# Sliding-window attention in blocks of 64 queries by 192 keys, late scores in the projections' banks, and other ends of the program

## The chip, the cores and the metric

One core of a Trainium2 chip runs the whole program. The metric is device microseconds (us) of one execution; lower is better. Engines are named as in the profile: PE does matmuls and transposes (PEld is its weight load), DVE and ACT the elementwise work, POOL a little elementwise work and some DMA issues, SP most DMA issues. The inputs and outputs lie in DRAM; PE writes into PSUM banks, everything else that is worked on lies in SBUF.

## What is computed

A step of a two-layer decoder in fp32, for a prompt of 1024 tokens and for 8 single tokens with caches (1032 columns in all, model width 1024). Layer 0 is gated linear attention beside attention into 256 memory tokens, then a squared-ReLU MLP. Layer 1, in which most of the change lies, is sliding-window attention beside memory attention, then the MLP. Its core, cut:

```
nb = L // WINDOW                                   # WINDOW = 128, L = 1024: 8 blocks
qb = q.reshape(B, nb, WINDOW, 4, 3, 64)            # 12 query heads on 4 key heads of 64
kk, vv = band_keys(k), band_keys(v)                # each block sees itself and the block before: 256 keys
qi = arange(WINDOW)[:, None] + WINDOW; kj = arange(2 * WINDOW)[None, :]
dist = qi - kj
band = (dist >= 0) & (dist < WINDOW)               # a query sees the 128 keys that end with its own
s = q . k / 8 + bias[dist], -inf outside the band
m = max(max_k s, sink);  p = exp(s - m);  p = p / (sum_k p + exp(sink - m));  o = p . v
```

A query in the first half of a block of 128 can see only the first 192 of the 256 keys, one in the second half only the last 192. The single tokens attend to a cache of 127 keys and their own, and the cache, shifted by one, is also an output.

## The kernel before, in words

Work is laid out with features on partitions and tokens on columns; the 1032 tokens go in three chunks `c` (`CH`: 384, 384 and 264 columns). A projection (`proj`, matmul at L248) is done in three fp32r products of high and low parts; `mmps` hands out its PSUM banks ("mm", "mx"). A scheduler sets the order on each engine from the priorities written in the code (`first()` raises one by 400) and from when buffers come free.

Layer 1's window attention is `swa(t, i2)` (L1713 to L1773): `t` counts 6 pairs of heads, `i2` 4 pairs of 128-token blocks, 24 calls, here called units and written (t, i2). A unit has: four score matmuls of 64 rows by 128 columns with 256 keys each (L1726) into the double bank `sA`, of which there is one; on DVE four `tensor_tensor_reduce` that add the bias and take the maximum into `z` (L1730), and small ones (L1735, L1737); on ACT the sink's exponential (L1740) and four exponentials (L1745); the sum and its reciprocal (L1747, L1749) and one multiplication of 128x1024 (L1751) on DVE; eight transposes on PE into `sT` (L1758, one buffer); their copy `pt` on ACT (L1760); eight matmuls with the values `vtok` into bank `sf` (L1769, "PV" below); one copy into `q` on ACT (L1773). A trace shows an fp32 matmul as two passes, so that L1769 is x16 and L1726 x8. Units with i2 = 0 have no block before their first one, and leave out a quarter of this.

The loop (L1865 to L1877) calls `in_b(t)`, the query projection for pair t (L1704, 72 matmuls), before the four units of pair t, and `in_b(5)` before those of pair 3. So from pair 4 on no projection is left to fill PE between units. From unit (4, 2) on, each unit is preceded by a step of `swa_dec` (L1775), the single tokens' attention: its loads from POOL's queue (L1780 to L1784, L1806, L1808), the shifted copy of the key and value caches from DRAM to DRAM (L1785, L1786), the memory attention's loads (L444) and scores (L454), window scores (L1817) and values (L1846). After the units come the output projection (L496 on) and layer 1's MLP.

At the start of the program the first chunk of `xT` and the first weights are loaded (L1019, L214), normalised and split (L1030, L1031, L152), for the first projection matmuls (L248). At its end, `down_plain` (L976) does the MLP's second half; `Residual` collects each chunk's sum of squares, and its `finish` (L286) makes the factor `rf` (L192, the statistics' matmul L198, ACT, L207 to L209), then in four pieces j multiplies by it (L320), adds the residual that was loaded from `xd` (L322) and stores (L323).

## Time and profile before

| | us |
|---|---|
| median of 3 runs | 2208.44 |
| lowest and highest | 2204.39, 2211.3 |
| the profiled execution's own time | 2209.21 |
| its span in the trace | 2207.4 |
| PE busy | 2152.1 (97%) |
| DVE, ACT, POOL busy | 1504.0, 1061.5, 109.4 |

The span is the time from the first to the last recorded instruction of the profiled execution; its own time is 1.8 us more. Times within the trace count from the span's start. A busy share is a mean over stages that have different limits, so the stages are read one by one below.

### The profile page before, as it was taken

The page shows a single profiled execution, that of the slowest core. Times are in us where ns is not written, and L with a number is a line of the kernel's source. Part 1 is how long each engine was busy: PE and PEld are TensorE (multiplying, and loading weights), DVE is VectorE, ACT ScalarE, POOL GpSimd, SP SyncE. Part 2 cuts the span into 40 slices and gives each one's busy share as a digit, 9 for nine tenths or more (in the row PEclk, how much of TensorE's full clock was granted, in tenths as well). Part 3 has the DMA queues.
Part 4 walks back from the last instruction along what each step waited for, and adds up shares of the span by engine and source line. Part 5 has one row for each costly group of instructions (what it writes and reads, how often), then busy time and mean ns, then how long its engine had stood idle before and what let it go on. Part 6 is the DMA issues. An engine that isn't in the chain of part 4 may idle for free.

```text
span 2207.4 us, 40137 instructions
## 1 busy us (share of the span) xinstructions
PE 2152.1 (97%) x16250; PEld 2054.4 (93%) x16250; DVE 1504.0 (68%) x2811; ACT 1061.5 (48%) x2071; POOL 109.4 (5%) x123
## 2 busy tenths in 40 slices
PE   7999999999999999999999999799999999999996
PEld 5879999999999999999999778599999999999996
DVE  6656647768877777666478465647887776856557
ACT  6354536557644554334334365646654544433433
POOL 0002000000000002520000000100000000000010
PEclk9999999999999999999999999899999999999998
DMA  5512016543644459574334101324364337635422
GB/s 186 161 63 80 24 64 168 163 131 106 200 157 159 138 196 337 176 256 128 111 95 140 48 20 40 106 73 145 112 219 158 128 138 264 220 112 167 149 88 78
DMA packets 134687, 303.68 MB, mean 138 GB/s; under 512 B 11033, under 2 KB 65489, under 8 KB 134209
## 3 DMA queue, kind: packets, MB, share of 16 engines
q1 hardware_dynamic: 116736, 258.80, 36.0%
q0 software_dynamic: 7824, 29.44, 3.8%
q10 hardware_dynamic: 9936, 12.81, 1.6%
q8 instruction: 129, 2.11, 0.4%
q14 instruction: 62, 0.51, 0.1%
HBM read 213.57 MB, written 89.51 MB: 137 GB/s over the span
## 4 chain that ended last, share of the span: by engine, by line
PE 84%; DVE 4%; ACT 2%; DMA 2%; issue 1%; DVEq 0%; ACTq 0%
PE mm L248 15%; PE mx L248 7%; PE mx L756 6%; PE mx L758 6%; PE mx L757 6%; PE mx L921 4%; PE mx L923 4%; PE mx L922 4%; PE mm L756 3%; PE mm L758 3%; PE mm L757 3%; PE mm L922 2%; PE mm L921 2%; PE mm L923 2%; PE sx L921 1%; PE sf L922 1%
## 5 line engine op out<-in xcount | busy, mean ns | idle before, releaser
L152 ACT CAST wh<-ws 128x512 fp32r<-128x512 f32 (+1 forms) x262 | 188.3, 726 | 319.7 <-DVE ws L605 105.7
L153 DVE TENSOR_TENSOR wl<-ws,wh 128x512 fp32r<-128x512 f32 (+1 forms) x262 | 213.7, 822 | 122.8 <-ACT wh L152 121.7
L756 PE MATMUL mx<-xf,wh 128*128 128x258 f32 x1048 | 297.1, 283 | 0.0
L758 PE MATMUL mx<-xf,wl 128*128 128x258 f32 x1048 | 295.9, 282 | 0.0
L757 PE MATMUL mx<-xf,wh 128*128 128x258 f32 x1048 | 295.7, 282 | 0.0
L248 PE MATMUL mm<-xh,wh 128*128 128x384 f32 (+1 forms) x864 | 282.0, 326 | 0.8 <-ACT xh L152 0.5
L248 PE MATMUL mm<-xh,wl 128*128 128x384 f32 (+1 forms) x864 | 278.9, 323 | 0.0
L248 PE MATMUL mm<-xl,wh 128*128 128x384 f32 (+1 forms) x864 | 278.7, 323 | 0.0
L152 ACT CAST wh<-wr 128x1024 fp32r<-128x1024 f32 x98 | 103.0, 1051 | 315.3 <-PE sx L922 300.3
L153 DVE TENSOR_TENSOR wl<-wr,wh 128x1024 fp32r<-128x1024 f32 x98 | 119.8, 1223 | 173.7 <-ACT wh L152 173.7
L921 PE MATMUL mx<-sa,wh 128*128 128x258 f32 x784 | 221.6, 283 | 1.1 <-DVE aw L594 1.1
L922 PE MATMUL mx<-sa,wh 128*128 128x258 f32 x784 | 220.6, 282 | 0.0
L923 PE MATMUL mx<-sa,wl 128*128 128x258 f32 x784 | 220.5, 282 | 0.0
L757 PEld LDWEIGHTS mx<-xf,wh 128*128 128x128 f32 x1048 | 198.1, 189 | 0.4
L756 PEld LDWEIGHTS mx<-xf,wh 128*128 128x128 f32 x1048 | 197.7, 189 | 0.4
L758 PEld LDWEIGHTS mx<-xf,wl 128*128 128x128 f32 x1048 | 197.9, 189 | 0.0
L248 PEld LDWEIGHTS mm<-xh,wh 128*128 128x128 f32 x864 | 163.0, 189 | 10.8 <-issue 6.3
L248 PEld LDWEIGHTS mm<-xh,wl 128*128 128x128 f32 x864 | 162.6, 188 | 7.4 <-issue 5.4
L248 PEld LDWEIGHTS mm<-xl,wh 128*128 128x128 f32 x864 | 163.2, 189 | 6.5 <-issue 5.5
L921 PEld LDWEIGHTS mx<-sa,wh 128*128 128x128 f32 x784 | 147.5, 188 | 1.6 <-DVE aw L594 1.5
L922 PEld LDWEIGHTS mx<-sa,wh 128*128 128x128 f32 x784 | 148.4, 189 | 0.0
L923 PEld LDWEIGHTS mx<-sa,wl 128*128 128x128 f32 x784 | 148.1, 189 | 0.0
(542 smaller groups left out, 5749.6 us busy)
## 6 DMA issues: line engine op xcount, KB each, us to landing
ra<-awd SPq DMA_DIRECT2D x98, 516.0 KB, 3.9
ws<-in_w_up SPq DMA_DIRECT2D x64, 512.0 KB, 6.1
wr<-in_w_downb SPq DMA_DIRECT2D x56, 512.0 KB, 5.6
awd<-aw SPq DMA_DIRECT2D x26, 1032.0 KB, 6.8
awd<-am SPq DMA_DIRECT2D x28, 774.0 KB, 8.3
ws<-in_w_in_a SPq DMA_DIRECT2D x20, 512.0 KB, 3.6
xd<-f ACTq DMA_DIRECT2D x24, 384.0 KB, 4.8
ws<-in_w_out SPq DMA_DIRECT2D x16, 512.0 KB, 3.5
```

Source lines behind the costliest of these rows:

```text
L152: nc.scalar.copy(hi, src)
L153: (eng or nc.vector).tensor_tensor(lo, src, f32(hi), ALU.subtract)
L248: mm = nc.tensor.matmul(ps[:M, :n], w_[:, k, :M], x_[:, k, :], start=(i == 0), stop=(i == 3 * KT - 1))
L756: nc.tensor.matmul(ps, wh(k), xh, start=(k == 0), stop=False)
L757: nc.tensor.matmul(ps, wh(k), xl, start=False, stop=False)
L758: mm = nc.tensor.matmul(ps, wl(k), xh, start=False, stop=(k == n - 1))
L921: nc.tensor.matmul(ps, wh[:, q, ms], h, start=(jj == 0 and q == 0), stop=False)
L922: nc.tensor.matmul(ps, wh[:, q, ms], lo, start=False, stop=False)
L923: mm = nc.tensor.matmul(ps, wl[:, q, ms], h, start=False, stop=end)
```

## The change

1. A unit works on blocks of 64 queries by 192 keys. Its scores are eight matmuls of 64 rows by 64 columns with 192 keys each, on the four quarters (j, b) of the array, where j is the head and b the half of the block; the reductions, exponentials and the multiplication take 192 columns in place of 256; there are six transposes in place of eight, and `pt` is 768 wide. The values are applied by eight matmuls of 128 rows by 64 columns and eight of 64 by 64, each with 64 moving columns, into two banks (`sf` and `sx`), and two copies bring them to `q`. A copy of the values shifted by 64 tokens, `vsh`, is made once by a memset and two DMAs from POOL's queue. The bias table is laid out for it on the host.
2. For t of 4 and 5 and even i2 the scores go into two of the projections' banks (`mm`) in place of `sA`.
3. The steps of `swa_dec` begin at (4, 0), and the two cache shifts are tied behind the loads.
4. `load_memkv` of layer 1 uses two buffers of the pool `tq`.
5. `xd` and `xT` become one tensor for each chunk.
6. For the last chunk of the last layer the priority is 4000 in place of 400 (`urgent`), and its `rf` has the buffer `r0` in place of the single `rf`; for the middle chunk the adds of pieces 1 and 3 go to POOL.

```
-    xd = dram.tile([P, KT, NT], F32, tag="xd", name="xd")
+    xd = [dram.tile([P, KT, n], F32, tag=f"xd{c}", name=f"xd{c}") for c, (_, n) in enumerate(CH)]
...
+    def urgent(c):
+        return tc.high_priority(400 if c < 2 else 4000)
...
-            rf = rp.tile([P, 384], F32, tag="rf", name=nm("rf"))[:, :n]
+            rf = rp.tile([P, 384], F32, tag="r0" if self.last and self.c == 2 else "rf", name=nm("rf"))[:, :n]
...
-                    TT(f[:, ks, :], f[:, ks, :], xs, ALU.add)
+                    eng = nc.gpsimd if self.c == 1 and j % 2 else nc.vector
+                    eng.tensor_tensor(f[:, ks, :], f[:, ks, :], xs, ALU.add)
...
-                load_split(xl, hl, A["xT"][:, :, c0 : c0 + n], n, r, G_MIXPRE, (2, 3, 4)[c] * 3 * KT * 384,
+                load_split(xl, hl, A[f"xT{c}"], n, r, G_MIXPRE, (2, 3, 4)[c] * 3 * KT * 384,
...
-                z = ap.tile([P, 2, 2, 256], F32, tag="z", name=nm("z"))
+                z = ap.tile([P, 2, 2, 192], F32, tag="z", name=nm("z"))
...
-                ps = psS().rearrange("p (j u k) -> p j u k", j=2, u=2)
+                if t >= 4 and i2 % 2 == 0:
+                    ps = [mmps(), mmps()]
+                else:
+                    ps = psS()
+                    ps = [ps[:, :512], ps[:, 512:]]
...
+                    for b in range(2):
+                        q0 = (2 * i2 + u) * P + 64 * b
+                        for j in range(2):
+                            rows, cols = slice(64 * j, 64 * j + 64), slice(64 * b, 64 * b + 64)
+                            spans = [(0, 192, q0 - P)]
+                            if lo[u]:
+                                spans = [(64, 128, 0), (128, 192, 0)] if b == 0 else [(64, 192, 0)]
+                            for c0, c1, k0 in spans:
+                                row(nc.tensor.matmul(ps[j][cols, u, c0:c1], q[rows, t, q0 : q0 + 64],
+                                                     kf[rows, pr, k0 : k0 + c1 - c0], start=True, stop=True))
...
-                TT(z3, z3, rs.unsqueeze(2).to_broadcast([P, 4, 256]), ALU.mult)
+                TT(z3, z3, rs.unsqueeze(2).to_broadcast([P, 4, 192]), ALU.mult)
...
+                        row(nc.tensor.transpose(tps[:, o : o + P], z[:, j, u, 64 * u : 64 * u + P], ident))
+                for j in range(2):
+                    zj = z[:, j].rearrange("p u k -> p (u k)")
+                    row(nc.tensor.transpose(tps[:, (4 + j) * P : (5 + j) * P], zj[:, P : 2 * P], ident))
...
-                po = psO()
+                po = [stps("sf"), stps("sx")]
...
+                            v = vsh[:, i, c] if b != u else vtok[:, i - 1 + u, c]
+                            gather(j, u, b, v, pt[:, 2 * j + u, 64 * b : 64 * b + 64], False)
...
+                            v = vtok[part, i - u, c] if b == u else vsh[part, i + 1 - 2 * u, c]
+                            gather(j, u, b, v, pt[part, 4 + j, 64 * b : 64 * b + 64], b == 1)
...
-                nc.gpsimd.dma_start(vc[WIN - 1 : WIN], vdec)
-                nc.gpsimd.dma_start(O["swa_ks"][:, : WIN - 1, :], A["swa_k_nat"][:, 1:, :])
-                nc.gpsimd.dma_start(O["swa_vs"][:, : WIN - 1, :], A["swa_v_nat"][:, 1:, :])
+                own = nc.gpsimd.dma_start(vc[WIN - 1 : WIN], vdec)
+                for o, src in (("swa_ks", "swa_k_nat"), ("swa_vs", "swa_v_nat")):
+                    shift = nc.gpsimd.dma_start(O[o][:, : WIN - 1, :], A[src][:, 1:, :])
+                    tc.add_manual_dep(shift.ins, own.ins.name, NOSYNC, reason="behind the loads")
...
-            kt, vt = load_memkv(ap, 1)
+            vsh = ap.tile([P, NB, 256], F32, tag="vsh", name="vsh", bufs=1)
+            nc.gpsimd.memset(vsh[:64, 0], 0.0)
+            nc.gpsimd.dma_start(vsh[64:], vtok[:64])
+            nc.gpsimd.dma_start(vsh[:64, 1:], vtok[64:, : NB - 1])
+            room = [view(tp.tile([P, 768], F32, tag="tq", name=nm("mkv")), [P, 2, MEM]) for _ in range(2)]
+            kt, vt = load_memkv(ap, 1, room)
...
-                    if (t, i2) >= (4, 2):
+                    if t >= 4:
                         next(dec, None)
```

Three places show how this moves instructions. The first is PE where the last projection of `in_b` ends. Rows are line, operation, output and inputs with buffer numbers, and the tile; before, two PVs (into `sf`) and one group of transposes (`sT`) of pair 3 follow the last L248, among the scores of pair 4:

```order
L248 MATMUL mm_16297<-xh_14185,wl_16242 128x264
L1726 MATMUL sA_16326<-kf,q 128x128 x2
L1726 MATMUL sA_16326<-kf,q 128x256
L1769 MATMUL sf_16183<-pt_16181,vtok_14265 64x128 x8
L1758 MATMUL sT_16218<-ident,z_16193 128x128 x8
L1726 MATMUL sA_16326<-kf,q 128x256
L1790 MATMUL sx_16442<-ident,kf 8x128 x2
L1769 MATMUL sf_16229<-pt_16227,vtok_14265 64x128 x8
L1726 MATMUL sA_16368<-kf,q 128x256 x4
L454 MATMUL sx_16505<-ar_16414,ar_16412 32x256
```

In the changed kernel (L251 is the projection, L1740 the scores) the last projection is followed by scores alone, of unit (4, 0) in two `mm` banks and of (4, 1) in `sA`:

```order
L251 MATMUL mm_16511<-xh_14187,wl_16456 128x264
L1740 MATMUL mm_16587<-kf,q 64x64
L1826 MATMUL sx_16567<-ident,kf 8x128 x2
L1740 MATMUL mm_16587<-kf,q 64x64
L1740 MATMUL sA_16707<-kf,q 64x192
L1740 MATMUL mm_16588<-kf,q 64x64 x2
L1740 MATMUL mm_16587<-kf,q 64x128
L1740 MATMUL mm_16588<-kf,q 64x128
```

The scores of (4, 2), (4, 3) and two pieces of (5, 0) follow, and only then the first transposes of (4, 0). A little further on PE has this, where L1774 and L1777 are the transposes of (4, 1), L1785 the PV of (4, 0), and L458 the single tokens' memory scores (L454 before), which take the keys from the arena `ar`:

```order
L1785 MATMUL sx_16627<-pt_16624,vtok_14267 64x64 x2
L1774 MATMUL sT_16734<-ident,z_16705 128x128 x4
L1777 MATMUL sT_16734<-ident,z_16705 128x128 x2
L458 MATMUL sf_16644<-ar_16539,ar_16537 32x256
L1740 MATMUL sA_16997<-kf,q 64x192
L458 MATMUL sf_16644<-ar_16538,ar_16537 32x256 x2
```

The transposes of (4, 2) and the PV of (4, 1) stand behind these scores. ACT at the same place: `z_16705` belongs to (4, 1), `z_16772` to (4, 2), `sT_16617` to (4, 0), so that the exponentials of (4, 1) and the first of (4, 2) (L1762) stand ahead of the copy `pt` of (4, 0) (L1779):

```order
L1762 ACTIVATE z_16705,sm_16725<-z_16705,sm_16720 128x192 x3
L1762 ACTIVATE z_16772,sm_16793<-z_16772,sm_16788 128x192
L1779 COPY pt_16624<-sT_16617 128x768
L1757 ACTIVATE sm_16790<-sm_16790 128x4
L1762 ACTIVATE z_16772,sm_16793<-z_16772,sm_16788 128x192 x3
L1808 COPY q<-sf_16626 128x128
```

The exponentials moved one to two units ahead of the copies in the first units of pair 4; in those of pair 5 a unit's `pt` stands ahead of the next unit's exponentials again, or among them.

The second place is POOL's queue. Before, the two cache shifts stand at the start of the program:

```order
L2012 UNCONDITIONAL_BRANCH
L1785 DMA out_swa_ks<-in_swa_k_nat 8x2x16256
L1192 MEMSET vtok 1x4x256
L1786 DMA out_swa_vs<-in_swa_v_nat 8x2x16256
L1193 MEMSET vtok 1x8
```

Now they stand behind the single tokens' loads, late in layer 1:

```order
L448 DMA ar_16537<-in_mem_kT 128x512 x2
L448 DMA ar_16538<-in_mem_kT 128x512 x4
L1819 DMA ar_16540<-vdec_14257 1x8x256
L1821 DMA out_swa_ks<-in_swa_k_nat 8x2x16256
L1821 DMA out_swa_vs<-in_swa_v_nat 8x2x16256
L1831 MEMSET ar_16540 128x512
L1833 MEMSET ar_16540 128x256
L1844 DMA ar_16537<-in_dec_sink 128x1
L448 DMA ar_16537<-in_mem_v 128x512 x2
```

Ahead of the values `in_mem_v` and behind the keys `in_mem_kT` there are now two transfers more.

The third place is the end of the program on DVE. Before (`f_24591` is the middle chunk, `f_24595` the last one), the last chunk's `rf` (L192) stands behind the middle chunk's work:

```order
L996 TENSOR_TENSOR f_24595<-mx_25056,acc_21698 128x132
L320 TENSOR_TENSOR f_24591<-f_24591,rf_24907 128x768 x2
L322 TENSOR_TENSOR f_24591<-f_24591,xall_24916 128x768 x2
L320 TENSOR_TENSOR f_24591<-f_24591,rf_24907 128x768
L192 TENSOR_TENSOR rf_25074<-tq_24963 128x264
L322 TENSOR_TENSOR f_24591<-f_24591,xall_24916 128x768
L207 TENSOR_TENSOR sf_25076<-sf_25076,rf_25074 128x264
L208 SCALAR_TENSOR_TENSOR sf_25076<-sf_25076,rf_25074 128x264
L209 SCALAR_TENSOR_TENSOR rf_25074<-sf_25076,rf_25074 128x264
L320 TENSOR_TENSOR f_24595<-f_24595,rf_25074 128x528 x2
```

Now (`f_24913` the middle chunk, `f_24917` the last) L195 makes it ahead of the last two adds of the matmuls' results, and the middle chunk's work fills the time until the factor is there:

```order
L195 TENSOR_TENSOR rf_25396<-tq_25285 128x264
L1000 TENSOR_TENSOR f_24917<-mx_25378,acc_22018 128x132
L1000 TENSOR_TENSOR f_24917<-mx_25378,acc_22020 128x132
L326 TENSOR_TENSOR f_24913<-f_24913,xall_25238 128x768
L323 TENSOR_TENSOR f_24913<-f_24913,rf_25229 128x768 x2
L210 TENSOR_TENSOR sf_25398<-sf_25398,rf_25396 128x264
L326 TENSOR_TENSOR f_24913<-f_24913,xall_25238 128x768
L211 SCALAR_TENSOR_TENSOR sf_25398<-sf_25398,rf_25396 128x264
L323 TENSOR_TENSOR f_24913<-f_24913,rf_25229 128x768
L212 SCALAR_TENSOR_TENSOR rf_25396<-sf_25398,rf_25396 128x264
L323 TENSOR_TENSOR f_24917<-f_24917,rf_25396 128x528 x2
```

Two adds of the middle chunk have left DVE for POOL, and the last chunk's factor no longer waits for the middle chunk's.

## Rows read from the trace of the kernel before

**Rows 1.** The page of the profile: the busy times of the engines over the whole span, and of its DMA issues the first projection's weights (KB each, median us from issue to landing).

```profile
PE 2152.1 (97%) x16250; PEld 2054.4 (93%) x16250; DVE 1504.0 (68%) x2811; ACT 1061.5 (48%) x2071; POOL 109.4 (5%) x123
...
ws<-in_w_in_a SPq DMA_DIRECT2D x20, 512.0 KB, 3.6
```

**Rows 2.** The windows view, by stage: stretch in us and its length, busy time (and instructions) of PE, PEld, DVE, ACT and POOL, the granted clock of PE (1.00 is 2.4 GHz, 0.50 is 1.2 GHz), the DMA share, GB/s. 1281 to 1357 are the units of the first pairs, 1378 to 1441.5 those behind the last projection.

```profile
40.00:1228.00 1188.00, 1178.54 (x8776) 1142.93 (x8775) 827.13 (x1501) 560.91 (x1093) 84.40 (x75) 1.00 0.44 145
...
1281.00:1357.00 76.00, 74.06 (x588) 60.66 (x588) 45.60 (x168) 43.90 (x137) 0.93 (x3) 1.00 0.06 21
...
1378.00:1441.50 63.50, 50.31 (x438) 33.58 (x436) 44.85 (x164) 39.09 (x108) 10.57 (x21) 0.89 0.30 98
```

**Rows 3.** The timeline of the first 16 us: start, duration, engine, line and operation, and in brackets the idle time before it and what ended that.

```profile
1.36 0.74 POOL L1785 DMA_DIRECT2D out_swa_ks<-in_swa_k_nat  x1 [0.91 <-POOLq L2005]
...
11.70 1.04 ACT L152 CAST wh<-ws 128x1024 fp32r<-128x1024 f32 x1 [5.05 <-DMA ws<-in_w_in_a]
...
14.13 0.69 PE L248 MATMUL mm<-xh,wh 128*128 128x384 f32 x1
```

**Rows 4.** The DMA view of the first 32 us: POOL's queue (packets, MB, share of the 16 engines' time), and issues with their KB and median us to landing.

```profile
q0 software_dynamic: 48, 1.04, 8.0%
...
ws<-in_w_in_a SPq DMA_DIRECT2D x3, 512.0 KB, 8.1
...
out_swa_ks<-in_swa_k_nat POOLq DMA_DIRECT2D x1, 1016.0 KB, 9.3
```

**Rows 5.** The timeline of PE, 1343 to 1347.5: one unit's PV among projection matmuls.

```profile
1344.94 1.09 PE L1769 MATMUL sf<-pt,vtok 128*64 128x128 f32 x16
1345.96 0.44 PE L248 MATMUL mm<-xl,wh 128*128 128x384 f32 x1
1346.24 0.33 PE L248 MATMUL mm<-xh,wl 128*128 128x384 f32 x1
```

**Rows 6.** The timeline of PE, 1378 to 1442: the last projection matmul, a unit's scores, the same on the lower clock, the single tokens' memory scores and their window scores (four column tiles of 128x32 side by side).

```profile
1378.56 0.28 PE L248 MATMUL mm<-xh,wl 128*128 128x264 f32 x1
...
1383.94 1.13 PE L1726 MATMUL sA<-kf,q 64*128 64x256 f32 x8
...
1387.95 2.07 PE L1726 MATMUL sA<-kf,q 64*128 64x256 f32 x6 [1.95 <-DVE sm L1730]
...
1395.58 0.64 PE L454 MATMUL sx<-ar,ar 128*32 128x256 f32 x2
...
1405.48 1.08 PE L1817 MATMUL sf<-ar,ar 128*32 128x128 f32 x32
```

**Rows 7.** The lines view by form, 1228 to 1442: busy us, mean ns of one, and the idle time before them with what ended most of it.

```profile
L1745 ACT ACTIVATE z<-z,sm 128x256 f32<-128x256 f32 x84 | 41.8, 500 | 18.5 <-DVE sm L1737 11.3 <-DVE sm L1735 7.2
L1730 DVE CUSTOM_DVE_ANT_0 z<-sA,bias,sinks 128x256 f32<-128x256 f32 x84 | 37.6, 477 | 22.4 <-PE sA L1726 22.4
...
L1751 DVE TENSOR_TENSOR z<-z,sm 128x1024 f32<-128x1024 f32 x24 | 29.3, 1221 | 0.5
...
L1760 ACT COPY pt<-sT 128x1024 f32<-128x1024 f32 x18 | 18.1, 1008 | 18.2 <-PE sT L1758 18.2
...
L1760 ACT COPY pt<-sT 128x768 f32<-128x768 f32 x6 | 4.8, 799 | 10.3 <-PE sT L1758 10.3
...
L1745 ACT ACTIVATE z<-z,sm 128x128 f32<-128x128 f32 x12 | 4.7, 394 | 3.3 <-DVE sm L1735 2.9 <-DVE sm L1737 0.4
```

**Rows 8.** The chain of waits, 1357 to 1442 (start, us, what): one round of a late unit, from its transposes to the next unit's.

```profile
1409.41 1.08 PE sT L1758 x8
1410.57 1.01 ACT pt L1760
...
1412.07 1.38 ACT z L1745 x6
...
1413.95 1.24 DVE z L1751
1415.23 0.88 PE sT L1758 x6
```

**Rows 9.** The timeline of POOL, 1357 to 1442: the issue of the single tokens' memory keys.

```profile
1379.72 3.19 POOL L444 DMA_DIRECT2D ar<-in_mem_kT  x6
```

**Rows 10.** The timeline of the last 24 us, all engines: the last add of the matmuls' results, the last chunk's last scaling, the middle chunk's last multiplication, the last chunk's factor `rf` and its statistics, and its multiplications and adds.

```profile
2188.10 0.49 DVE L996 TENSOR_TENSOR f<-mx,acc 128x132 f32<-128x132 f32 x2
...
2189.07 0.51 ACT L281 ACTIVATE f<-f,gains 128x264 f32<-128x264 f32 x1
...
2191.98 0.95 DVE L320 TENSOR_TENSOR f<-f,rf 128x768 f32<-128x768 f32 x1
2192.96 0.43 DVE L192 TENSOR_TENSOR rf<-tq 128x264 f32<-128x264 f32 x1
...
2193.45 1.25 PE L198 MATMUL sf<-rf,ones 128*128 128x264 f32 x2 [5.62 <-DVE rf L192]
...
2194.49 1.97 PE L198 MATMUL sf<-t,ones 128*128 128x264 f32 x4
...
2198.78 1.33 DVE L320 TENSOR_TENSOR f<-f,rf 128x528 f32<-128x528 f32 x2
...
2202.50 1.32 DVE L322 TENSOR_TENSOR f<-f,xall 128x528 f32<-128x528 f32 x2
```

**Rows 11.** The lines view by form of the whole span: POOL's elementwise products of 128x1024 (mean ns of one).

```profile
L237 POOL TENSOR_TENSOR wf<-wf,gains 128x1024 f32<-128x1024 f32 x12 | 44.2, 3682 | 62.6 <-DMA wf<-in_w_in_b 37.5 <-DMA wf<-in_w_kv 25.1
```

More of the change, by code (lines that the diff above doesn't have):

```diff
@@ L270, in feed @@
             if self.last:
-                with first():
+                with urgent(self.c):
                     self.feed_last(m)
@@ L978, in down_plain @@
             c0, n = CH[c]
[L979 removed]
+            R[c] = Residual(c, F[c], G_FFNPOST + l, xd[c], last=(l == 1), floor=X[c][1])
             for m in range(KT):
@@ L989, in down_plain @@
                 tick(mm, 3 * NPL * n)
-                with first():
+                with urgent(c) if l else first():
                     if c < 2:
@@ L1634, in hybrid_decoder_step @@
                         make_o0(0, oh0)
-            X = out_proj(0, make_o0, svp, so, ff, A["xT"], False, oh0)
+            X = out_proj(0, make_o0, svp, so, ff, [A[f"xT{c}"] for c in range(3)], False, oh0)
         pmd.close()
@@ L1714, in swa @@
                 pr = t // 3
-                z = ap.tile([P, 2, 2, 256], F32, tag="z", name=nm("z"))
+                z = ap.tile([P, 2, 2, 192], F32, tag="z", name=nm("z"))
                 m4 = small(4, P, "w1")
+                lo = [64 if (i2 == 0 and u == 0) else 0 for u in range(2)]
                 if i2 == 0:
-                    nc.gpsimd.memset(z[:, :, 0, :P], 0.0)
-                lo = [P if (i2 == 0 and u == 0) else 0 for u in range(2)]
-                ps = psS().rearrange("p (j u k) -> p j u k", j=2, u=2)
+                    nc.gpsimd.memset(z[:, :, 0, :64], 0.0)
@@ L1721, in swa @@
+                if t >= 4 and i2 % 2 == 0:
[3 more added lines that the diff above has]
+                    ps = [ps[:, :512], ps[:, 512:]]
+                ps = [view(x, [P, 2, 192]) for x in ps]
                 row = Row()
                 for u in range(2):
-                    i = 2 * i2 + u
-                    for j in range(2):
-                        rows = slice(64 * j, 64 * j + 64)
-                        row(nc.tensor.matmul(ps[:, j, u, lo[u] :], q[rows, t, i * P : i * P + P],
-                                             kf[rows, pr, i * P - P + lo[u] : i * P + P], start=True, stop=True))
+                    for b in range(2):
[8 more added lines that the diff above has]
+                                                     kf[rows, pr, k0 : k0 + c1 - c0], start=True, stop=True))
@@ L1755, in swa @@
                     for u in range(2):
-                        for kt_ in range(lo[u] // P, 2):
-                            o = (4 * j + 2 * u + kt_) * P
-                            row(nc.tensor.transpose(tps[:, o : o + P], z[:, j, u, kt_ * P : kt_ * P + P], ident))
-                pt = ap.tile([P, 2, 4, P], F32, tag="pt", name=nm("pt"), bufs=2)
-                nc.scalar.copy(pt[:, :, lo[0] // P :, :],
-                               tps.rearrange("p (j a b) -> p j a b", j=2, a=4)[:, :, lo[0] // P :, :])
@@ new lines, in swa, with gather @@
+                po = [stps("sf"), stps("sx")]
+                row = Row()
+                begun = set()
+                def gather(j, u, b, v, p_, last):
+                    row(nc.tensor.matmul(po[u][64 * j : 64 * j + 64, 64 * b : 64 * b + 64], v, p_,
+                                         start=((j, u) not in begun), stop=last))
+                    begun.add((j, u))
+                for b in range(2):
+                    for u in range(2):
+                        i = 2 * i2 + u
+                        if lo[u] and b == 0:
+                            continue
+                        for j in range(2):
+                            c = slice(64 * (2 * pr + j), 64 * (2 * pr + j) + 64)
+                            v = vsh[:, i, c] if b != u else vtok[:, i - 1 + u, c]
+                            gather(j, u, b, v, pt[:, 2 * j + u, 64 * b : 64 * b + 64], False)
@@ L1765, in swa @@
                     i = 2 * i2 + u
-                    for kt_ in range(lo[u] // P, 2):
-                        for j in range(2):
-                            kvh = 2 * pr + j
-                            row(nc.tensor.matmul(
-                                po[64 * j : 64 * j + 64, u * P : u * P + P],
-                                vtok[:, i - 1 + kt_, 64 * kvh : 64 * kvh + 64],
-                                pt[:, j, 2 * u + kt_, :], start=(kt_ == lo[u] // P), stop=(kt_ == 1)))
-                nc.scalar.copy(q[:, t, i2 * 2 * P : (i2 + 1) * 2 * P], po[:, : 2 * P])
+                    nc.scalar.copy(q[:, t, i * P : i * P + P], po[u][:, :P])
```

38 lines of the change are left out of this document (27 added, 11 removed).

## The prediction, written before the changed kernel was timed

> **What bounds the kernel now.** I read the page first: PE is busy 97% of the span, DVE 68%, ACT 48% [rows 1]. So only time on PE, or holes in PE, can move the end, and I read the windows by stage for the holes [rows 2]. From 40 to 1228 us PE is busy 1178.5 of 1188 us: what the start gains is handed on to the end, and nothing the change does to DVE, ACT or the DMAs there counts. The units of pairs 0 to 3 (1281 to 1357) have PE busy 74.1 of 76 us: there the price is PE's. Behind the last projection (1378 to 1441.5) PE is busy 50.3 of 63.5 us at a mean granted clock of 0.89, with DVE at 44.9 and ACT at 39.1: no engine is full, a chain through all three is the bound.
>
> The chain of waits shows a late unit's round: transposes start at 1409.41, `pt` 1.01, exponentials, multiplication 1.24, and the next transposes start at 1415.23, so 5.8 us a unit [rows 8]. It is a ring because ACT copies `pt` before the next unit's exponentials, and those must end before the next transposes.
>
> **Start.** The first projection matmul runs at 14.13, and the weights it needs are cast at 11.70, as soon as they land [rows 3]. These weights took 8.1 us to land [rows 4], against 3.6 over the whole run [rows 1]. In between lies the key cache's shift, issued at 1.36 and landed 9.3 us later [rows 3, 4]; it took 8.0% of the sixteen queues' 32 us, 2.6 us, all ahead of 11.70. The change sends it late. Taken out: -2.5 us (bounds -1, if the loads' issue limits them, and -4, as the `xT` rows are also longer pieces).
>
> **Units while PE is the bound (pairs 0 to 3, 16 units).** No row shows a 64x64 tile. The nearest rows are two tiles side by side and, in the single tokens' scores, four: 32 passes of 128x32 tiles in 1.08 us, about a quarter of what they would take in a row [rows 6]. I take four at a time.
> - Scores: before, eight passes of 213 ns, two by two, 0.85 us and a tail, 1.13 in all [rows 6]. Now sixteen of 160 ns (192/256 of it), four by four, 0.64: -0.2.
> - Transposes: eight take 1.08, six 0.88 [rows 8]: -0.2, but nothing in the four units with i2 = 0, which have six already.
> - PV: before, 16 passes of 108 ns two by two, 0.87 and a tail, 1.09 [rows 5]. Now the 128x64 half is 16 passes of 54 by twos, 0.43, and the 64x64 half 16 by fours, 0.22: -0.2. The new form within PV costs a switch: on the way back to projections the first matmul takes 0.44 in place of 0.33 and starts the next 0.1 late [rows 5], so about +0.2. Sum 0.
>
> That is -0.4 for twelve units and -0.2 for four: **-5.6 us**. The Trainium skill (TensorEngine Tiling (Array Packing), Key Properties) speaks against this change: "Mode switching requires drain", any change of the tiling mode empties PE. The rows above show such a price, 0.1 to 0.2 us each; the changed order has 175 runs of one tile form where there were 146, so by that rule alone 3 to 6 us would be given back, of which the sum already holds about 0.2 for each unit.
>
> The exponentials, `pt`, the multiplication and the second copy to `q` are hidden by PE here: ACT is busy 43.9 of 76 us [rows 2], and the change takes more off it than it adds. The per-chunk `xd` and `xT`, `room`, the memset and two DMAs for `vsh` (POOL is idle and the DMAs have hundreds of us) cost nothing under the same cover; without it, a microsecond or two each.
>
> **Behind the last projection.** It ends at 1378.84 [rows 6]. In the order before, two PVs and one group of transposes of pair 3 come after it; now none do. So it ends at 1378.8 - 5.6 + 2 x 1.09 + 1.08 = 1376.5, with eight whole units to come.
> - Round: exponentials 4 x 50 ns less (between 500 and 394 [rows 7]), -0.2; `pt` 1008 to 799 [rows 7], -0.2; multiplication of 768 columns 0.95 (the same form in the tail [rows 10]) for 1.22 [rows 7], -0.27; transposes -0.2. 5.8 becomes 4.9. The reductions, 477 for 256 columns [rows 7], get shorter off the ring.
> - Scores of (4, 0) to (4, 3) now run ahead, in `mm` and `sA` by turns, and ACT's order has exponentials of later units ahead of `pt`. That opens the ring for pair 4, but the single tokens' steps now begin there too, so I take 4.9 for all.
> - First unit to its transposes some 6 us (scores 0.9, reductions 1.4, exponentials and small ones 2.4, multiplication 1), seven rounds of 4.9, and transposes, `pt` and PV 2.8: 43.1. Last PV ends at 1419.6 in place of 1441.5, the end of this stage [rows 2]: **-21.9 us** for both stages.
>
> Bounds: -10 to -28 (the second and third rival).
>
> **End.** Before, the last chunk's `rf` (2192.96) waits until the middle chunk has multiplied with the one buffer (2191.98), and PE's statistics, idle 5.6 us, run on the lower clock, 3.0 us [rows 10]; then 2.3 us to the first multiplication at 2198.78, and eight operations to 2203.82. Now `rf` precedes the last adds. The last scaling ends at 2189.6 [rows 10]; statistics on the full clock 1.5 and the same 2.3 us give the factor by 2193.4. On DVE five operations of 0.95 and three of 0.45 stand between the last add of PE's results (2188.6 [rows 10]) and the last chunk's eight: 2194.7, so DVE binds, and 5.0 us more give 2199.7: **-4.1 us** (bounds -2 and -5). POOL's two adds, at 768/1024 of 3682 ns [rows 11] 2.8 us each, are hidden: the second ends near 2197. If POOL took 6 us for one, the end would be POOL's and some 3 us of this would go.
>
> **Sum:** -2.5 - 21.9 - 4.1 = -28.5 us from the profiled execution's own 2209.2 us, which is 0.8 above the median: 2180.7, so **2181 us**.
>
> **Rivals.**
> 1. Late units run ahead freely. For: the order above. Against: pair 5 has the old order on ACT, and `sT` is single. A unit would then cost ACT's work alone, exponentials 1.6, `pt` 0.8 and some 0.8 for the rest, and the waits of a round, an estimated 4.1 us: -6, 2175 us.
> 2. The single tokens' keys stop PE. Their scores now stand before the transposes of (4, 2) and the PV of (4, 1), so these wait with them. Before, the keys were issued at 1379.72 [rows 9] and the scores ran at 1395.58 [rows 6], 17 us after the last projection; the same offset gives 1393.3, where the first two units would be through by 1388.3: 5 us of idle PE. Idling 1.95 us at 1387.95 was followed by six score passes in 2.07 us, the lower clock [rows 6]: 1 us a unit for two or three. Two shifts of 2.6 us of all queues each may delay the loads as well. +5 to +13: about 2190 us.
> 3. 64x64 tiles run only two at a time. Scores +0.4 and PV +0.2 against no gain: no -5.6, about +4 in the 16 units, PE not binding later: 2192 to 2198, say 2196 us. For: only column tiles are seen by fours. Against: nothing.
> 4. The other side, slower: quarters of the array run one after another. Scores 16 x 0.16 = 2.56 in place of 0.64, PV 32 x 0.054 = 1.73 in place of 0.65: +3.0 a unit over the forecast. Against it, the two row halves and two or four column tiles overlap now. The scores and PV alone would be +72 on 24 units, some 15 of it in late holes of PE: 2181 + 57, about 2238 us. From 1.2 us a unit over the forecast (28.5/24) the change loses.
> 5. It does nothing: the late stage takes a new wait of equal size (a bank `mm` that the single tokens or the output projection also want). 2203 to 2212 us.
>
> **How the numbers follow.** Forecast 0.48, rival 1 0.14, rival 2 0.18, rival 3 0.11, rival 4 0.05, rival 5 0.04. The first four are all faster than the old time by over 0.3% (6.6 us, about what a measurement of this kernel can tell from no change): 0.91; rival 5 is mostly no change: 0.04; slower: 0.05. The range reaches from rival 1 with the better bound of the start and the end (2175 less 4) to past rival 3: 2171 to 2198 us, and leaves out rivals 4 and 5 and the ends of the others.
>
> **What would show it.** Start: the weights landing in under 6 us, first projection matmul near 11.6. Units: scores x16 in about 0.9 us, PV in two groups, together 1.1, transposes x6 0.85; the last projection near 1374 (1376.5 less the start). Late: rounds of 4.9 us, PE busy over 85% from there, last PV near 1417. End: statistics by 1.5 us, right behind the matmuls, DVE full to its end. I am wrong if score groups take over 1.3 us, if PE waits for the keys over 3 us, or if the last PV comes more than 50 us after the last projection.

## The result and the profile after

The changed kernel takes 2185.07 us (median; 2183.23 to 2190.3) against 2206.68 for the one before: the ratio is 0.9905, 95% interval 0.989 to 0.9921, so 21.6 us or 1% less. The forecast was 2181. A second set of runs (`again`, below) gave the same median and 0.9899.

The first profile is of the longest of its four runs, 2190.3 us; the second one of a run of 2181.7. I read both, since they differ by more than some parts of the change are worth. The page of the first, busy times:

```profile
PE 2143.8 (98%) x16814; PEld 2047.8 (94%) x16814; DVE 1492.9 (68%) x2809; ACT 1054.5 (48%) x2095; POOL 117.0 (5%) x128
```

The same matmuls of both traces, set side by side, show where the 19 us between the two profiled executions were gained. At 30 us the changed kernel is 4.8 us ahead, at 120 us 2.0, at 1200 us 2.5; behind the window attention 15.2; from 1861 on 16.8; at the end 18.9. In the second profile the same points read 5.8 (at 60 us), 6.0, 7.6, 23.8, 25.4 and 27.5.

**Start.** The timeline, first 16 us, and the DMA view of the first 32 us answer to [rows 3, 4]:

```profile
8.39 1.04 ACT L155 CAST wh<-ws 128x1024 fp32r<-128x1024 f32 x1 [1.63 <-DMA ws<-in_w_in_a]
...
10.81 0.69 PE L251 MATMUL mm<-xh,wh 128*128 128x384 f32 x1
...
ws<-in_w_in_a SPq DMA_DIRECT2D x3, 512.0 KB, 6.4
```

The weights land 3.3 us earlier, and so does the first projection; 2.5 were forecast.

**A unit.** PE's timeline of the first profile (PV of one unit, scores and transposes of another), answering to [rows 5, 6, 8]:

```profile
1345.38 0.34 PE L1785 MATMUL sf<-pt,vtok 128*64 128x64 f32 x4
...
1346.00 0.27 PE L1785 MATMUL sf<-pt,vtok 64*64 64x64 f32 x2
...
1346.24 0.23 PE L1785 MATMUL sx<-pt,vtok 64*64 64x64 f32 x2
...
1354.19 0.88 PE L1740 MATMUL sA<-kf,q 64*64 64x192 f32 x16
...
1358.09 0.63 PE L1774 MATMUL sT<-ident,z 128*128 128x128 f32 x4 [0.38 <-DVE z L1768]
1358.56 0.38 PE L1777 MATMUL sT<-ident,z 128*128 128x128 f32 x2
```

Sixteen score passes end 0.88 us after their start: four quarters work at a time, as taken (0.64 and a tail). Transposes take 0.85, PV 1.09 (1345.38 to 1346.47), as before: sum 0, as forecast. Its second half starts 0.1 us late, the price of the second form.

**Behind the last projection.** The windows view, first profile, from the last projection matmul to the last PV:

```profile
1374.90:1426.10 51.20, 42.50 (x580) 28.05 (x578) 37.58 (x159) 33.29 (x112) 11.66 (x23) 0.87 0.44 155
```

62.6 us, 3.3 of them work of pair 3 that now stands ahead of the last projection, have become 51.2; 43.1 were forecast. The forms, 1228 to 1430, answering to [rows 7]:

```profile
L1762 ACT ACTIVATE z<-z,sm 128x192 f32<-128x192 f32 x84 | 37.3, 448 | 11.9 <-DVE sm L1754 7.8 <-DVE sm L1752 4.0
L1748 DVE CUSTOM_DVE_ANT_0 z<-sA,bias,sinks 128x192 f32<-128x192 f32 x72 | 27.5, 408 | 12.8 <-PE sA L1740 12.7
...
L1768 DVE TENSOR_TENSOR z<-z,sm 128x768 f32<-128x768 f32 x24 | 22.9, 954 | 0.2
L1779 ACT COPY pt<-sT 128x768 f32<-128x768 f32 x24 | 19.2, 800 | 22.0 <-PE sT L1777 21.9
```

The exponentials (447 by interpolation), the multiplication (950) and the copy (799) are what the prediction took; the reductions it did not price. The terms of the round were right; what failed is what stands ahead of the first round and between the rounds.

**End.** The timeline of the first profile, answering to [rows 10]:

```profile
2171.53 1.32 PE L201 MATMUL sf<-t,ones 128*128 128x264 f32 x4
...
2173.60 2.29 POOL L326 TENSOR_TENSOR f<-f,xall 128x768 f32<-128x768 f32 x1 [58.02 <-DVE f L323]
...
2174.49 2.21 DVE L326 TENSOR_TENSOR f<-f,xall 128x768 f32<-128x768 f32 x1
...
2178.04 1.80 POOL L326 TENSOR_TENSOR f<-f,xall 128x768 f32<-128x768 f32 x1 [2.15 <-issue]
...
2178.29 2.74 DVE L323 TENSOR_TENSOR f<-f,rf 128x528 f32<-128x528 f32 x2
...
2183.43 1.31 DVE L326 TENSOR_TENSOR f<-f,xall 128x528 f32<-128x528 f32 x2
```

The statistics follow the matmuls at once, on the full clock. But two DVE operations are long: an add that takes 0.95 elsewhere takes 2.21, a pair of 1.31 takes 2.74. They end at 2176.70 and 2181.03, 0.8 and 1.2 us behind POOL's adds (2175.89 and 2179.84): about the usual time of one operation, and of a pair.

### The profile page after: what moved, and what is told of

Same layout as the page of the kernel before. It is cut to its first block, busy times and chain, and to the rows that moved or that the text cites. A ratio compares the mean times of both kernels' runs of the same rounds, so it can differ in the third digit from the quotient of the medians.

```text
span 2188.5 us, 41306 instructions
## 1 busy us (share of the span) xinstructions
PE 2143.8 (98%) x16814; PEld 2047.8 (94%) x16814; DVE 1492.9 (68%) x2809; ACT 1054.5 (48%) x2095; POOL 117.0 (5%) x128
## 4 chain that ended last, share of the span: by engine, by line
PE 90%; DVE 4%; ACT 3%; DMA 2%; issue 1%; SPq 0%; DVEq 0%; ACTq 0%
PE mm L251 17%; PE mx L251 8%; PE mx L760 6%; PE mx L762 6%; PE mx L761 6%; PE mx L925 4%; PE mx L927 4%; PE mx L926 4%; PE mm L762 3%; PE mm L760 3%; PE mm L761 3%; PE mm L925 2%; PE mm L926 2%; PE mm L927 2%; PE sx L925 1%; PE sf L926 1%
## 5 line engine op out<-in xcount | busy, mean ns | idle before, releaser
L156 DVE TENSOR_TENSOR wl<-ws,wh 128x512 fp32r<-128x512 f32 (+1 forms) x262 | 213.5, 821 | 105.2 <-ACT wh L155 103.9
L251 PE MATMUL mm<-xh,wh 128*128 128x384 f32 (+1 forms) x864 | 282.2, 327 | 0.5 <-ACT xh L155 0.4
L251 PE MATMUL mm<-xh,wl 128*128 128x384 f32 (+1 forms) x864 | 279.2, 323 | 0.0
L251 PE MATMUL mm<-xl,wh 128*128 128x384 f32 (+1 forms) x864 | 278.3, 322 | 0.0
L156 DVE TENSOR_TENSOR wl<-wr,wh 128x1024 fp32r<-128x1024 f32 x98 | 119.8, 1223 | 175.9 <-ACT wh L155 175.9
L251 PEld LDWEIGHTS mm<-xh,wh 128*128 128x128 f32 x864 | 162.9, 189 | 10.4 <-issue 7.0
L251 PEld LDWEIGHTS mm<-xl,wh 128*128 128x128 f32 x864 | 162.9, 189 | 7.2 <-issue 6.3
L251 PEld LDWEIGHTS mm<-xh,wl 128*128 128x128 f32 x864 | 162.5, 188 | 6.8 <-issue 4.9
```

The lines of the kernel that those rows point to most:

```text
L156: (eng or nc.vector).tensor_tensor(lo, src, f32(hi), ALU.subtract)
L251: mm = nc.tensor.matmul(ps[:M, :n], w_[:, k, :M], x_[:, k, :], start=(i == 0), stop=(i == 3 * KT - 1))
```

## Experiments

My theory of the missing 8 us behind the last projection was at first the single tokens' steps, which now begin at (4, 0); its rival the order of the first units, with a clock that falls while PE waits. Most of the rest undo one part each; a median is of four to six runs. This table has what each profiled execution shows (us; "stage" runs from the last projection matmul to the last PV, "end" from the last MLP matmul to the end of the span).

| kernel | median | ratio to before, interval | first projection | stage, mean granted clock | end |
|---|---|---|---|---|---|
| before | | | 14.13 | 62.6, 0.89 | 19.9 |
| changed, first profile | 2185.07 | 0.9905, 0.989 to 0.9921 | 10.81 | 51.2, 0.87 | 17.7 |
| again | 2185.07 | 0.9899, 0.9884 to 0.9914 | 9.38 | 47.8, 0.93 | 17.7 |
| dec_later | 2191.44 | 0.9923, 0.9909 to 0.9937 | 9.52 | 50.0, 0.86 | 18.3 |
| no_mm_scores | 2197.19 | 0.9955, 0.9939 to 0.9971 | 9.18 | 59.8, 0.86 | 17.6 |
| blocks128 | 2193.05 | 0.9933, 0.992 to 0.9946 | 10.08 | 54.4, 0.94 | 17.6 |
| shift_first | 2186.75 | 0.9912, 0.9891 to 0.9934 | 13.79 | 45.9, 0.93 | 17.5 |
| dve_adds | 2183.07 | 0.9892, 0.9873 to 0.9911 | 9.95 | 46.0, 1.00 | 16.5 |
| old_end | 2187.7 | 0.9912, 0.9893 to 0.9931 | 8.86 | 47.5, 0.93 | 19.9 |
| dec_41 | 2186.67 | 0.9905, 0.9884 to 0.9926 | 9.32 | 49.9, 0.90 | 18.3 |
| blocks64_only | 2197.01 | 0.996, 0.9946 to 0.9973 | 13.78 | 51.8, 0.93 | 19.9 |
| queries_early | 2183.43 | 0.9894, 0.9879 to 0.9909 | 9.38 | 46.9, 0.93 | 16.4 |
| dve_adds_2 | 2186.05 | 0.9905, 0.989 to 0.992 | 9.81 | 46.8, 0.93 | 16.4 |
| no_single | 2174.84 | 0.9856, 0.9832 to 0.9881 | 8.70 | 39.3, 0.96 | 17.6 |

### again: the changed kernel once more

> The changed kernel unchanged, for a second profile and as the base of the others on the same chip: 2184 us (2182 to 2191). In the first profile PE ran on the lower clock around 100 to 108 us and at two places behind the last projection (1385 to 1391 and 1402 to 1408), and 51.1 us lay between the last projection matmul and the last PV, where 43.1 were forecast. Theory A: these clock drops come and go with the execution, so they fall elsewhere here, and the 51.1 us get 2 to 5 us shorter. Rival B: they belong to the order of the work, and 51 us come again within 1 us.

The stage took 47.8 us where the first profile has 51.2, with the same order of work; and `dve_adds`, which differs only at the program's end, 46.0 in its profile. The windows view of `again` and of `dve_adds`:

```profile
1369.80:1417.50 47.70, 39.54 (x576) 27.48 (x578) 37.58 (x159) 33.20 (x112) 11.63 (x23) 0.93 0.47 166
```

```profile
1371.40:1417.40 46.00, 36.90 (x580) 25.53 (x578) 37.44 (x159) 32.98 (x113) 11.66 (x23) 1.00 0.48 172
```

PE's busy time falls with the length, 42.5, 39.5 and 36.9, DVE's does not: the difference goes with the granted clock, 0.87, 0.93 and 1.00. The mean clock alone does not set it: with the same order of work `dve_adds_2` has 46.8 and `old_end` 47.5 us at 0.93. Theory A holds: up to 5 us of a run come and go here. How the stage begins, in the chain of waits of `again`:

```profile
1369.95 1.05 ACT wh L155
1371.03 1.23 DVE wl L156
1372.26 0.26 DVE z L1748
...
1374.97 0.15 DVE ar L442 x2
...
1377.29 0.88 DVE z L1768
1378.30 1.08 PE sT L1774 x4
```

The first transposes start 8.3 us behind the last projection, where 6 were forecast. DVE first splits a weight of the output projection (L156, held up by its cast on ACT), then does the reductions of three units and copies of the single tokens, and only then the first multiplication (L1768): in the first 10.3 us it is busy 9.7, and PE 6.7:

```profile
1369.70:1380.00 10.30, 6.73 (x88) 4.67 (x91) 9.66 (x48) 5.73 (x24) 7.16 (x14) 0.87 1.02 340
1380.00:1390.00 10.00, 10.00 (x118) 6.26 (x118) 6.24 (x29) 7.69 (x31) 2.68 (x6) 0.79 0.68 268
...
1410.00:1418.00 8.00, 6.92 (x94) 6.03 (x93) 7.69 (x12) 7.86 (x22) 0.00 (x0) 1.00 0.01 2
```

The full engine changes: DVE first, then PE, at the end DVE and ACT (which split the output projection's inputs between the last units).

The other traces bound what makes the first unit late. Its transposes start 8.3 us behind the last projection in `dec_later` too, 8.2 in `blocks64_only` and 7.5 in `no_mm_scores`. In the last two no scores go to `mm`, so running ahead costs 0.8 us at most. The weight's split stands ahead of the first reduction in all of them, and that reduction starts 2.1 us behind the last projection, where the forecast had 0.9 for the scores. No run moves the split, so its share is not shown.

### dec_later, dec_41: when the single tokens' steps begin

```
-                    if t >= 4:
+                    if (t, i2) >= (4, 2):        # dec_41: (4, 1)
                         next(dec, None)
```

> One part undone: the single tokens' steps begin at (4, 2) again, everything else as in the changed kernel. Theory A: these steps, put into the first units of pair 4, are what took the gain of the run-ahead (the window scores now use bank sx, which the units' PV needs as well, and the memory scores stand before the transposes of (4, 2)); without them there the stage behind the last projection is 4 to 8 us shorter, about 2178 us. Rival B: the time went to the first units themselves (three units' reductions ahead of the first multiplication, PE idle and then on the lower clock), and the single tokens' steps only end later: same to 4 us slower, 2184 to 2188 us.

> The single tokens' steps begin at (4, 1), between the change's (4, 0) and the old (4, 2). In the changed kernel the PV of (4, 1) waits 4 to 5 us for bank sx, which the single tokens' window scores hold until their queries are copied on DVE and their reduction is done; here that PV stands ahead of them. Theory A: this wait was on the path; 3 to 4 us faster, 2181 to 2182 us, 44 us from the last projection to the last PV. Rival B: the single tokens' chain sets the end of the stage, and each step later costs time, as with (4, 2): 2187 to 2189 us.

Later was slower for (4, 2): 2191.44, 6.4 us over `again`; for (4, 1) the time is not told apart from the change's, and the stage is 49.9 us. My theory fell for both, and `dec_later` was slower than its rival had it as well: the single tokens' steps are not better kept out of the first units. In the chain of `dec_later` they stand between the last units instead:

```profile
1409.70 2.73 PE sf L458 x32
1412.43 0.86 PE sx L1882 x16
1413.29 0.59 PE sT L1774 x4
```

and less of the output projection runs in the stage (560 matmuls of all kinds in it, 576 in `again`): from the last PV to the last MLP matmul it is 747.9 us here, 744.7 in `again`.

### no_mm_scores: all scores in sA

```
-                if t >= 4 and i2 % 2 == 0:
+                if False:
```

> One part undone: all scores in the one bank sA, everything else as in the changed kernel. Theory A: the scores in the projections' banks let pair 4 run ahead, so without them 3 to 6 us are lost, 2187 to 2190 us. Rival B: running ahead only moved the reductions of three units ahead of the first multiplication and let PE cool; without it the time is the same or 2 us less, 2182 to 2185 us.

12.1 us slower than `again`, twice theory A's. PE's waits in that stage, summed by what it waited for (total, times, longest), show the ring of [rows 8] again:

```profile
PE sT L1774 <- DVE z L1768: 5.9, 4, 3.0
PE sA L1740 <- DVE sm L1748: 5.6, 3, 2.3
```

In `again` the wait of transposes for the multiplication is not among PE's nine largest. With `blocks64_only` there are all four combinations, by the stage: sA alone and steps from (4, 2) 51.8, from (4, 0) 59.8; scores in `mm` and steps from (4, 2) 50.0, from (4, 0) 46.0 to 51.2. So the late scores are worth little with late steps, and the early steps cost 8 us without the late scores: the two parts work only together. This is one profile for most of the four, each at its own clock, and `blocks64_only` lacks the other parts of the change too.

### blocks128 and blocks64_only: the blocks out of the change, and alone

`blocks128` has the old body of `swa` (128 queries by 256 keys), with its scores in `mm` as in the change; `blocks64_only` is the kernel before with the new body, `vsh`, the bias table and `room`.

> One part undone: blocks of 128 queries by 256 keys as before (four score matmuls, eight transposes, eight values' matmuls into one bank, one copy), with the late scores still in the projections' banks and all other parts of the change. Theory A, from the trace of the changed kernel (scores of a unit 0.88 us where they took 1.13, transposes 0.85 for 1.08, PV 1.1 for 1.09): 0.3 to 0.4 us of PE for each of 16 units and 0.6 to 0.9 us for each of the last eight, so 10 to 13 us slower, 2194 to 2197 us. Rival B: behind the last projection other things set the end, and only PE's part counts: 4 to 6 us slower, 2188 to 2190 us.

> One part alone: the kernel before with the blocks of 64 by 192 (their bias table, vsh, and the two buffers of tq for the memory keys and values, without which vsh has no place). Scores stay in sA, the single tokens' steps begin at (4, 2), start, xd, xT and the program's end are as before. Theory A: the blocks are worth the same alone as within the change, where taking them out cost 8 us (some 2.6 in the units beside the projections, the rest behind them): 2198 to 2200 us. Rival B: behind the last projection their shorter operations only count once the late scores let the units run ahead: 2202 to 2205 us.

Taken out, the blocks cost 8.0 us, between the two theories; alone they gain 8.8 us (0.4%). In the traces of `blocks128` and the change the stretch from the first scores to the last projection is 101.56 and 99.00. But the two do not end it with the same work done: in `blocks128`, as before, two PVs and one group of transposes of pair 3 still follow the last projection. PE's timeline of `blocks128`:

```profile
1374.17 0.28 PE L251 MATMUL mm<-xh,wl 128*128 128x264 f32 x1
...
1375.45 1.09 PE L1778 MATMUL sf<-pt,vtok 128*64 128x128 f32 x16
1376.48 1.09 PE L1767 MATMUL sT<-ident,z 128*128 128x128 f32 x8
...
1378.78 1.09 PE L1778 MATMUL sf<-pt,vtok 128*64 128x128 f32 x16
```

So beside the projections the blocks are worth 2.56 and these 3.27 us, 5.8 in all; the 2.6 that the expectation of `blocks64_only` names leaves the second part out. Behind the last projection 54.4 us, less the 3.3, stand against 47.8 in `again` at nearly the same clock: 3.3 us more. Theory A of `blocks64_only` holds, with 1 us to spare: the blocks don't need the late scores.

### shift_first: the cache shifts at the start again

```
-                    shift = nc.gpsimd.dma_start(O[o][:, : WIN - 1, :], A[src][:, 1:, :])
-                    tc.add_manual_dep(shift.ins, own.ins.name, NOSYNC, reason="behind the loads")
+                    nc.gpsimd.dma_start(O[o][:, : WIN - 1, :], A[src][:, 1:, :])
```

> One part undone: the two cache shifts are free again, and stand at the start of POOL's queue as in the kernel before; the per-chunk xT stays. Theory A: the key shift shares the queues with the first loads, so the first projection matmul goes back from 9.4 to 10.8 (two profiles) to some 13 to 14 us, and the time is 2 to 4 us longer, 2187 to 2189 us. Rival B: the start's gain is from the longer pieces of xT; then the first projection stays near 10 us and the time within 1 us of 2185.

```profile
1.37 0.76 POOL L1821 DMA_DIRECT2D out_swa_ks<-in_swa_k_nat  x1 [0.92 <-POOLq L2050]
...
13.79 0.69 PE L251 MATMUL mm<-xh,wh 128*128 128x384 f32 x1
```

The first projection is back at 13.79: the start's gain is the shift's place, 3 to 5.1 us by the profiles. The longer pieces of `xT` show nothing, since `blocks64_only`, with the old `xT`, has 13.78. The whole time tells less: 2186.75, and an interval that overlaps the change's. Two things stand against the gain. The late stage is short here, 45.9 us at a clock of 0.93. And in the first profile of the change PE ran on the lower clock at 100 to 108 us, though busy, after 1.72 us of waiting (first row). The same work in `again`, 0.8 us earlier and after 1.40 us of waiting, did not (second row):

```profile
100.00:108.00 8.00, 7.66 (x26) 4.15 (x25) 2.31 (x3) 2.97 (x9) 0.00 (x0) 0.58 0.00 0
```

```profile
99.20:107.20 8.00, 7.21 (x42) 4.68 (x40) 4.70 (x7) 3.22 (x10) 0.00 (x0) 1.00 0.00 1
```

That took back 2.8 of 4.8 us. The wait alone does not bring it: before, PE waited 1.72 us at the same place, and the clock stayed at 1.00. Of the eleven profiles with the early start five show it (mean clock 0.7 to 0.8 from 95 to 112), of the three with the late start none so far down (before and `shift_first` 1.00, `blocks64_only` 0.90). Whether the early start brings it on isn't settled by so few.

### old_end, dve_adds, dve_adds_2: the end

`old_end` has the old priority, the single `rf` and all adds on DVE; `dve_adds` only the last:

```
-                    eng = nc.gpsimd if self.c == 1 and j % 2 else nc.vector
+                    eng = nc.vector
```

> The whole change of the program's end undone (priority, the buffer of the last chunk's factor, POOL's adds), everything else as changed. Theory A: the end behind the last matmul goes back from 17.7 to 19.9 us, 2 us slower, 2187 us. Rival B: the priority moves work of the last chunk before that too, and the forecast's 4 us are there: 2189 us.

> One part undone: the middle chunk's adds of pieces 1 and 3 go back from POOL to DVE; priority and buffer of the last chunk's factor stay as changed. Theory A: beside POOL's adds two DVE operations ran long (an add of 128x768 took 2.21 us where others take 0.95, a pair of 128x528 multiplications 2.74 for 1.31), 2.7 us lost, while the two adds cost DVE 1.9 us: 0.5 to 1 us faster, 2184 us, with the end behind the last matmul 17.0 for 17.7 us. Rival B: POOL's adds do unload DVE: 1 to 2 us slower, 2186 to 2187 us.

> The version with POOL's adds back on DVE once more, as the base of the one above on the same chip: 2183 us (2180 to 2185), 1 to 2 us under the changed kernel. In its first profile the clock stayed full behind the last projection, and the stage took 46.0 us; a lower mean clock here goes with a longer stage, about 1 us for each 0.02.

The last matmul, the statistics and the last operation of `old_end`, then the last matmul, the middle chunk's second add and the last operation of `dve_adds`:

```profile
2169.18 0.28 PE L992 MATMUL mx<-ah,wl 128*128 128x264 f32 x1
2175.08 1.25 PE L201 MATMUL sf<-rf,ones 128*128 128x264 f32 x2 [5.62 <-DVE rf L195]
...
2184.14 1.32 DVE L326 TENSOR_TENSOR f<-f,xall 128x528 f32<-128x528 f32 x2
```

```profile
2162.10 0.29 PE L992 MATMUL mx<-ah,wl 128*128 128x264 f32 x1
...
2165.78 0.95 DVE L326 TENSOR_TENSOR f<-f,xall 128x768 f32<-128x768 f32 x1
...
2174.38 0.71 DVE L326 TENSOR_TENSOR f<-f,xall 128x528 f32<-128x528 f32 x1
```

From the last matmul to the last operation's end these are 16.3 and 13.0 us. So priority and buffer bring 3.4 us (19.9 to 16.5 in the table), and POOL's adds take 1.2 back; priority and buffer were not taken apart. By the whole time `dve_adds` (0.9892, then 0.9905) can't be told from the change; the piece at the end was 16.5 and 16.4 in its two profiles and 17.7 in both of the change. The repeat came out at 2186.05, above what was expected of it, and its stage, 46.8 us at 0.93, does not follow the rule of 1 us for each 0.02, by which it would be 49.5.

The Trainium skill (SBUF — State Buffer, SBUF: two separate sides) has the rule: DVE and POOL share a port pair under "an exclusive lock, not a bandwidth split", which for a DVE operation of two SBUF inputs counts against a POOL operation that reads SBUF. The trace agrees: both long operations of DVE, 2.21 for 0.95 and 2.74 for 1.31 us, end about their own usual time after POOL's add, and in `dve_adds` none is long.

### queries_early: a version built from these

POOL's adds back on DVE; the single tokens' window queries are cleared on DVE and copied at a higher priority.

```
-                nc.gpsimd.memset(qmk, 0.0)
+                with tc.high_priority(400):
+                    nc.vector.memset(qmk, 0.0)
+                    ...
```

> A version built from the experiments so far: POOL's adds back on DVE, and the single tokens' window queries are cleared on DVE in place of POOL and copied at a higher priority, so that the window scores stand beside the memory scores, ahead of the PV of (4, 1), which waited 4 to 5 us for their bank. Theory A: that wait was on the path: 2 to 3 us faster than with POOL's adds undone alone (2183.1), 2180 to 2181 us. Rival B: DVE sets the pace of the first units (9.7 us busy in the first 10.3 us behind the last projection) and gets 1.5 us more to do there: same to 2 us slower, 2183 to 2185 us.

2183.43, the stage 46.9 us. The window scores begin 5.3 us earlier in the trace than in `dve_adds`, the last PV does not come earlier: rival B. The wait for bank `sx` was there but not what set the end. No version beats the change by more than the runs can tell.

### no_single: the late units alone

```
                 yield
+                return
                 next(mem)
                 ps = stps()
```

> The changed kernel without the single tokens' attention in layer 1: its loads, the cache outputs and the cleared buffers stay, but its scores, softmax, values and write-back are left out, as is the load of the memory values. Measured: how long the eight late units take alone, from the last projection matmul (46.0 us with the single tokens at full clock, 47.8 and 51.2 at a mean of 0.93 and 0.87). Theory A: the forecast's ring holds, 4.9 us a unit behind a first unit that starts 8.3 us late: 43 to 45 us, about 2183 us. Rival B: the ring is open, and the engines' own loads set the pace; the single tokens' work was in PE's and DVE's way: 4 us a unit, 34 to 38 us, about 2174 us.

The windows view of that stage:

```profile
1369.40:1408.90 39.50, 30.77 (x488) 22.42 (x486) 31.07 (x131) 30.80 (x106) 7.43 (x15) 0.96 0.44 152
```

Transposes of the eight units start at 1378.95 to 1406.01, 3.9 us apart on the mean; with the single tokens, in `again`, 1378.30 to 1414.74, 5.2. So the ring of 4.9 us no longer binds, as rival B had it, and the time is near its 2174 us. Its stage of 34 to 38 us did not come: it takes 39.3, with three engines busy 31 us each, so no engine's own load is the whole of it. The single tokens add 6.7 us (to 46.0 at full clock) to 8.5 (to 47.8 at 0.93). The first unit is no earlier without them, 9.3 us behind the last projection.

## Why the prediction was right, point by point

The direction, the size (21.6 against 28.5 us) and the range held; the terms did less well than the sum. The forecast counted from the profiled execution's 2209.2 us, and the median it was measured against is 2206.68. By the two profiles, the first 18.9 us and the second 27.5 us shorter, the stretch to 1200 us gave 2.5 and 7.6, units and late stage together 12.7 and 16.2 where 21.9 were forecast, the 1.6 below were not forecast, and the end gave 2.1. That the second profile comes within 1 us of 28.5 is luck. One of the prediction's signs of being wrong appeared in the first profile, where the last PV comes more than 50 us after the last projection; in the second it does not. PE is busy 83% of that stage in both, where over 85% were expected.

- **Start**, -2.5: the mechanism was right and the size low, 3.3 and 4.7 us at the first projection. What of it reaches the end isn't steady, 2.5 and 7.6 us at 1200 us in two profiles; `shift_first`, which starts only 0.3 us ahead of the kernel before, is 2.7 ahead there.
- **Units beside the projections**, -5.6: the prices of scores (0.88), transposes (0.85) and PV (1.09) were right, and so was four tiles at a time; rivals 3 and 4 fell with it. The sum came out: put into a kernel with the other parts, the blocks gain 5.8 us there (`blocks128`). The changes of tile form (in the traces, from 1215 us to the output projection, 146 runs of one form before and some 166 after) show no price beyond the 0.2 us a unit that the sum holds for them. Against the kernel before, counted from the key and value projections to the last projection, with the 3.3 us of pair 3's work that moved ahead of it, both profiles have 4.5. The difference is not the blocks': `blocks128`, with the old ones, loses 1.3 us of its lead over the kernel before in the same stretch. I did not look for its cause.
- **Behind the last projection**, 43.1 us: mis-sized by 2.9 at full clock (46.0), by 4.7 and 8.1 with the clock that the two profiles had. The failing step is the first unit, 8.3 for 6 us, where the forecast left out what else DVE does before the first multiplication, and that full clock was assumed; the round of 4.9 came out near (5.0 at full clock) for a wrong reason. The ring was opened: units alone take 3.9, and the single tokens' work, which the forecast put beside the ring at no cost, makes up the rest.
- **Rival 1** was that ring's opening, and true, but its 4.1 us a unit left out the single tokens. **Rival 2**: PE did not wait for the keys; the scores of the memory came at 1383.96 in `again` with no wait for a DMA. The lower clock came all the same in `again`, after PE had waited for DVE; in `dve_adds`, with the same order and PE busy 6.3 of the first 10.3 us, it did not come.
- **End**, -4.1: 2.2 (19.9 to 17.7). The priority and buffer brought 3.4, POOL's adds cost 1.2. The step that failed was "POOL's two adds are hidden": I looked at POOL's time and not at DVE's beside it. The row of 3682 ns misled as well, as a mean; its parts in the trace of before, two of twelve:

```profile
880.05 19.65 POOL L237 TENSOR_TENSOR wf<-wf,gains 128x1024 f32<-128x1024 f32 x1 [4.64 <-DMA wf<-in_w_kv]
...
908.78 1.89 POOL L237 TENSOR_TENSOR wf<-wf,gains 128x1024 f32<-128x1024 f32 x1 [4.18 <-DMA wf<-in_w_in_b]
```

- **Not forecast**: 1.6 us at 1859 us, where before PE waited for DVE and none of the changed kernels does, `blocks64_only` and `blocks128` among them. The one part of the change that these two share is `room`; no run undoes it alone, so the cause stays open.

## What to carry to other kernels

Where no engine is full, find the ring (which engine must do what before the next round can begin) and see whether a second buffer opens it; then add up every engine's own work in that stage, the side jobs too: here they cost 6.7 to 8.5 us that the forecast put at nothing. Test parts together as well as alone: the late scores and the early single-token steps are, by the stage, worth little or a loss apart, and more together than the sum. When two traces are compared up to a landmark, look which work stands on either side of it in each. A transfer that nobody waits for doesn't belong ahead of the first load, and an operation handed from DVE to POOL is priced on DVE's timeline.

## What of the hardware was not expected

- Four quarters of 64x64 do run together: sixteen passes of 192 columns in 0.88 us, against 1.13 for eight of 256 on two halves.
- Two-input adds on POOL held up two-input operations of DVE whole: 2.21 us for 0.95.
- The same order of work behind the last projection took 46.0, 47.8 and 51.2 us in three executions, at a mean granted clock of 1.00, 0.93 and 0.87, though PE's busy time in its first 10.3 us hardly differed (6.3 at 1.00, 6.7 at 0.93).
